# The FFN's first product as 2x2 block products: seven block multiplications for each pair of feature tiles instead of eight

## The chip, the cores and the metric

The kernel runs on one core of one Trainium2 chip. A core has TensorE (PE; its weight loads are listed apart as PEld), VectorE (DVE), ScalarE (ACT), GpSimd (POOL) and the queue SyncE (SP), which here only issues DMAs. The metric is the device time of one execution in microseconds; the median of three runs before the change is 1822.69 us (1821.99 to 1825.63).

## The reference, cut to what matters

Two layers, each a token mixer and then a gated ConvFFN, in float32, over 512 tokens of width 1024. The change touches the FFN's first product:

```
def conv_ffn(x, w_up, conv_w, conv_b, w_down):      # x 512x1024, w_up 1024x5632, w_down 2816x1024
    u = x @ w_up
    u = causal_conv_width_3(u, conv_w) + conv_b     # along the tokens, each feature by itself
    a, b = split(u, 2)
    return (gelu(a) * b) @ w_down
```

## The kernel before

Every float32 matrix product is made of three TensorE products of rounded halves: `split` (L143) writes a rounded high half with ACT (L144) and the rest, source minus high half, with DVE (L145); `mm3` (L147) issues the three matmuls (L149 to L151), each with its own 128x128 stationary tile and a moving operand of up to 512 columns.

Weights come as tiles of 128x1024 float32 (512 KB). `plan_all` (L300) writes their order into a list, `pump` (L125) walks it: it loads a tile into one of 3 `raw` buffers with a DMA on SP, splits it into one of 5 `w` buffers (`wsp`) at high priority, and `weight` (L137) keeps four tiles ready ahead of their use. The order of the instructions on each engine is then set by a list scheduler, by priorities and the dependences; each engine runs its own list in that order and waits where an operand isn't there.

In the FFN (`ffn`, L862) the activations lie transposed in `xT`: features on partitions, 8 tiles of 128 (the K tiles), high and low half, 512 tokens. The 5632 columns of `w_up` are 22 pairs of feature tiles (a tile of the gate's half `a`, and its partner of `b`). A tile is 8 K tiles x 3 matmuls of 512 columns into one PSUM bank (`fm_tile`, L153). The first two pairs run in two halves of 256 tokens, so that they can start before the mixer's last rows are normed. Then `up_pair` (L848) does `conv` (L839) on both tiles (ACT L843: last tap and bias; DVE L844 and L845: the two other taps, read from PSUM), gelu on ACT (L856), the product a*b on DVE (L857) and the split of the result into `gT` (a `u` tile, of which the pool `big` has 21). After 14 pairs the second product is done for these (28 tiles of `w_down`; PSUM added to `x` at L886), then come the other 8 pairs, then `closing` (L810) with the rest of `w_down` and the layer norm.

The lines that the prediction's steps touch: the weights' split (L144, L145), the conv (L843 to L845), the gate (L856, L857), the split of the gate (L144, L145), and the norm (L721, two DVE operands in SBUF, and L292, GpSimd's power of one or eight numbers).

## Time and profile before

| | |
|---|---|
| median of 3 runs | 1822.69 us |
| the profiled execution | 1823.07 us |
| its span, first to last instruction | 1821.4 us |
| granted TensorE clock, mean | 0.998 of 2.4 GHz |
| matmuls | 8286 |
| DVE, ACT, POOL instructions | 2205, 1187, 57 |

The profile is of one execution. Busy time is the union of an engine's instructions; matmuls overlap one another, so their pace is read from the starts of neighbours in the timeline, not from their durations. In a group of instructions the numbers behind the bar are busy us, mean ns of one, and the idle time of the engine just before them with what ended it.

### The profile page before, as it was taken

To read this page: it belongs to the slowest core of one execution; us is meant where nothing else is said; L and a number is where in the kernel's file an instruction comes from. 1 tells how busy PE (TensorE), PEld (TensorE's weight loads), DVE (VectorE), ACT (ScalarE), POOL (GpSimd) and SP (SyncE) were. 2 spreads that over 40 slices of the span, in tenths; PEclk is the share of its full clock that TensorE was granted. 3 is DMA by queue.
4 is the path that set the end of the run, shared out by engine and by line. 5 is a ranking of instruction groups with operands and counts; after the bars stand their busy time and mean duration, and the time that the engine had idled before them with its cause. 6 is when DMAs were issued, how large, how long until landed. Compare 5 with 4: busy or idle time off the path is not lost.

```text
span 1821.4 us, 21842 instructions
## 1 busy us (share of the span) xinstructions
PE 1796.6 (99%) x8286; PEld 1443.6 (79%) x8286; DVE 1183.5 (65%) x2205; ACT 791.4 (43%) x1187; POOL 35.5 (2%) x57
## 2 busy tenths in 40 slices
PE   9999999999999999999999999999999999999997
PEld 6787787888888888888777777778888888888885
DVE  6899867833496653356868997686335865633567
ACT  5744566622334442144356346574222354421441
POOL 0000000000000000000000000000000000000000
PEclk9999999999999999999999999999999999999999
DMA  5122231232452232232631222312325432223233
GB/s 193 64 70 70 70 105 57 66 109 81 137 211 93 94 97 97 94 93 93 210 127 59 70 70 79 96 56 72 105 93 193 131 116 93 93 93 95 96 113 135
DMA packets 57349, 186.17 MB, mean 102 GB/s; under 512 B 6710, under 2 KB 6966, under 8 KB 57244
## 3 DMA queue, kind: packets, MB, share of 16 engines
q1 hardware_dynamic: 51680, 170.74, 28.9%
q10 hardware_dynamic: 4284, 11.94, 1.8%
q0 software_dynamic: 1280, 2.10, 0.5%
q8 instruction: 65, 1.06, 0.2%
q14 instruction: 40, 0.33, 0.1%
HBM read 178.46 MB, written 4.19 MB: 100 GB/s over the span
## 4 chain that ended last, share of the span: by engine, by line
PE 84%; DVE 8%; DMA 3%; ACT 2%; issue 2%; POOL 1%; ACTq 0%; POOLq 0%; DVEq 0%; SPq 0%
PE ps L149 26%; PE ps L151 26%; PE ps L150 26%; DVE w L145 3%; PE ps L476 1%; PE ps L477 1%; ACT w L144 1%; DMA raw<-in_w_down 1%; PE ps L621 1%; POOL rs L292 1%; DMA raw<-in_w_mix_out 1%; DVE m L509 1%; DVE sc L510 1%; PE ps L631 0%; PE ps L728 0%
## 5 line engine op out<-in xcount | busy, mean ns | idle before, releaser
L145 DVE TENSOR_TENSOR w<-raw,w 128x1024 fp32r<-128x1024 f32 (+1 forms) x320 | 387.4, 1215 | 489.9 <-ACT w L144 489.1
L144 ACT CAST w<-raw 128x1024 fp32r<-128x1024 f32 (+1 forms) x320 | 331.8, 1042 | 526.6 <-PE ps L151 430.8
L149 PE MATMUL ps<-xT,w 128*128 128x512 f32 (+2 forms) x1232 | 477.0, 387 | 0.4 <-DVE xT L145 0.4
L151 PE MATMUL ps<-xT,w 128*128 128x512 f32 (+2 forms) x1232 | 473.2, 384 | 0.0
L150 PE MATMUL ps<-xT,w 128*128 128x512 f32 (+2 forms) x1232 | 473.1, 384 | 0.0
L149 PEld LDWEIGHTS ps<-xT,w 128*128 128x128 f32 (+1 forms) x1232 | 231.4, 188 | 48.7 <-DVE xT L145 1.6
L151 PEld LDWEIGHTS ps<-xT,w 128*128 128x128 f32 (+1 forms) x1232 | 231.2, 188 | 48.9
L150 PEld LDWEIGHTS ps<-xT,w 128*128 128x128 f32 (+1 forms) x1232 | 231.4, 188 | 45.9
L149 PE MATMUL ps<-w,u 128*128 128x512 f32 x480 | 190.6, 397 | 4.2 <-DVE u L836 2.6
L150 PE MATMUL ps<-w,u 128*128 128x512 f32 x480 | 189.6, 395 | 0.0
L151 PE MATMUL ps<-w,u 128*128 128x512 f32 x480 | 189.3, 396 | 0.0
L149 PE MATMUL ps<-w,xT 128*128 128x512 f32 x448 | 182.2, 407 | 1.9 <-DVE w L145 1.9
L150 PE MATMUL ps<-w,xT 128*128 128x512 f32 x448 | 178.0, 397 | 0.0
L151 PE MATMUL ps<-w,xT 128*128 128x512 f32 x448 | 177.6, 397 | 0.0
L144 ACT CAST u<-h 128x512 fp32r<-128x512 f32 x108 | 66.8, 621 | 199.8 <-DVE h L857 108.6
L149 PEld LDWEIGHTS ps<-w,u 128*128 128x128 f32 x480 | 90.4, 188 | 28.8 <-DVE u L836 4.3
L151 PEld LDWEIGHTS ps<-w,u 128*128 128x128 f32 x480 | 90.4, 188 | 20.9
L150 PEld LDWEIGHTS ps<-w,u 128*128 128x128 f32 x480 | 90.4, 188 | 20.3
L149 PEld LDWEIGHTS ps<-w,xT 128*128 128x128 f32 x448 | 84.5, 189 | 22.0 <-DVE w L145 2.3
L151 PEld LDWEIGHTS ps<-w,xT 128*128 128x128 f32 x448 | 84.4, 188 | 20.2
L145 DVE TENSOR_TENSOR u<-h,u 128x512 fp32r<-128x512 f32 x108 | 73.9, 687 | 38.0 <-ACT u L144 37.7
L150 PEld LDWEIGHTS ps<-w,xT 128*128 128x128 f32 x448 | 84.6, 189 | 16.3
(198 smaller groups left out, 2134.0 us busy)
## 6 DMA issues: line engine op xcount, KB each, us to landing
raw<-in_w_fm SPq DMA_DIRECT2D x160, 512.0 KB, 3.6
raw<-in_w_down SPq DMA_DIRECT2D x60, 512.0 KB, 3.5
raw<-in_w_tm SPq DMA_DIRECT2D x56, 512.0 KB, 3.5
raw<-in_w_mix_out SPq DMA_DIRECT2D x32, 512.0 KB, 3.6
raw<-in_p_attn SPq DMA_DIRECT2D x8, 512.0 KB, 3.5
u<-in_xT SPq DMA_DIRECT2D x8, 256.0 KB, 4.8
u<-u POOLq DMA_DIRECT2D x16, 128.0 KB, 2.7
u<-in_x ACTq DMA_DIRECT2D x4, 512.0 KB, 4.9
```

The lines of the kernel that those rows point to most:

```text
L144: self.nc.scalar.copy(hi, src)
L145: self.nc.vector.tensor_sub(lo, src, hi.bitcast(F32))
L149: mm(out, lh, rl, start=start, stop=False)
L150: mm(out, ll, rh, start=False, stop=False)
L151: mm(out, lh, rh, start=False, stop=stop)
L292: self.nc.gpsimd.tensor_tensor(r, ve, self.nhalf[:, :n], ALU.pow)
L476: mm(out, q, k, start=True, stop=False)
L477: mm(out, q, kl, start=False, stop=True)
L509: nc.vector.max(m8, sc)
L510: nc.vector.match_replace(sc, m8, sc, TAKEN)
L621: nc.tensor.transpose(ps[:, qb * 128:(qb + 1) * 128], P[qb][:, sb * 128:(sb + 1) * 128], self.ident)
```

## The change

From the third pair on (20 pairs in each layer), a pair's product is a 2x2 block product: the two blocks of rows are the halves of 256 tokens, the inner ones the halves of the 1024 features (4 K tiles each), the two blocks of columns the pair's two feature tiles. Strassen's scheme in Winograd's form makes it with seven products of sums and differences (`b11`, `t2`, `t1`, `t4`, `t3`, `b21`, `b22`), each 4 K tiles x 3 matmuls of 256 columns.

- `factors`: once in a layer, the sums and differences of the activations' blocks, on DVE and GpSimd, and their splits.
- `pair_weights`: a pair's weights come in one DMA of 1 MB; GpSimd makes four sums of 128x512 of them; one split of 128x512 and three of 128x1024 follow. The pair takes three `w` buffers and three `u` tiles.
- `pair_steps`: the seven products go into four PSUM banks; ACT (two copies) and DVE (five differences of 128x256, each with an operand in PSUM) put them together into `ua` and `ub` in SBUF. A pair's first product is issued before the last one of the pair ahead.
- `gate`: the conv's third tap is now a scaling in place on ACT and an add on GpSimd; the gate's low half is made by GpSimd (for the first two pairs, which stay as they were, by DVE).
- The second product runs in four pieces, after pairs 6, 12 and 16 (`down`) and at the end (`closing`), instead of two.
- `raw` is 2 buffers of two tiles each instead of 3 of one; two small scratch tiles of the mixer now come from the pool `half`.

```
 NFM = 36 + 2 * NF
-KA = 14
+DIRECT = 2
...
         self.tiny = pool("tiny", 6)
-        self.wraw = pool("wraw", 3)
+        self.wraw = pool("wraw", 2)
...
     def pump(self, ahead, parts=None):
-        while self.nsp < len(self.seq) and len(self.ready) < ahead:
+        while self.nsp < len(self.seq) and sum(c for _, _, c in self.ready) < ahead:
             key, src, n = self.seq[self.nsp]
             self.nsp += 1
-            raw = self.wraw.tile([128, n], F32, name=self.name("raw"), tag="raw")
+            if n == "pair":
+                self.ready.append((key, self.pair_weights(src), 3))
+                continue
+            raw = self.raw(n)
             self.nc.sync.dma_start(raw.rearrange(src[1], **src[2]) if src[1] else raw, src[0])
             w = self.wsp.tile([128, 2, n], F32R, name=self.name("w"), tag="w")
             with self.tc.high_priority():
                 for c in parts or (slice(0, n),):
                     self.split(w[:, 0, c], w[:, 1, c], raw[:, c])
-            self.ready.append((key, w))
+            self.ready.append((key, w, 1))
 
     def weight(self, key, keep=0):
         self.pump(4 + keep)
-        k, w = self.ready.pop(0)
+        k, w, _ = self.ready.pop(0)
         assert k == key, (k, key)
         return w
+    def pair_weights(self, src):
...
+        self.spare = None
+        raw = self.wraw.tile([128, 2, 1024], F32, name=self.name("raw"), tag="raw")
+        nc.sync.dma_start(raw, src)
+        b11, b21, b12, b22 = (raw[:, f, h * 512:(h + 1) * 512] for f in range(2) for h in range(2))
+        t, r = self.u(F32), self.u(F32)
+        one = self.u()
+        w = [self.wsp.tile([128, 2, 2, 512], F32R, name=self.name("w"), tag="w") for _ in range(3)]
+        with self.tc.high_priority():
+            add = nc.gpsimd.tensor_add
+            add(t[:, 0], b11, b12)
+            add(t[:, 1], t[:, 0], b22)
+            add(r[:, 0], t[:, 1], b21)
+            add(r[:, 1], b12, b22)
+            self.split(one[:, 0], one[:, 1], b11)
+            self.split(w[0][:, 0], w[0][:, 1], t)
+            self.split(w[1][:, 0], w[1][:, 1], r)
+            self.split(w[2][:, 0], w[2][:, 1], raw[:, :, 512:])
+        two = lambda x, j: (x[:, 0, j], x[:, 1, j])
+        return {"b11": (one[:, 0], one[:, 1]), "t1": two(w[0], 0), "t2": two(w[0], 1), "t4": two(w[1], 0),
+                "t3": two(w[1], 1), "b21": two(w[2], 0), "b22": two(w[2], 1)}
...
-        p = self.small([128, HEADS, 16], tag="ra", bufs=1)[:, :heads]
-        q = self.small([128, HEADS, 16], tag="rb", bufs=1)[:, :heads]
+        pq = self.h().rearrange("p (z h d) -> p z h d", z=4, h=HEADS)
+        p, q = pq[:, 0, :heads], pq[:, 1, :heads]
...
-        for m in range(2 * KA):
-            fm(FM["up"] + m)
-        for n in range(2):
...
+        for i in range(NF):
+            m = FM["up"] + 2 * i
+            if i < DIRECT:
+                fm(m)
+                fm(m + 1)
+            else:
+                P((l, "pair", i), a["w_fm"][l, m:m + 2].rearrange("m p c -> p m c"), "pair")
...
-        low = self.small([128, 512], tag="low", bufs=1)
+        low = self.h()
...
-    def conv(self, m, ps):
+    def conv(self, m, ps, also=None):
...
         nc.scalar.activation(c, ps, AF.Identity, scale=w[:, m, 2:3], bias=self.convb[:, m:m + 1])
         nc.vector.scalar_tensor_tensor(c[:, 1:], ps[:, :S - 1], w[:, m, 1:2], c[:, 1:], op0=ALU.mult, op1=ALU.add)
-        nc.vector.scalar_tensor_tensor(c[:, 2:], ps[:, :S - 2], w[:, m, 0:1], c[:, 2:], op0=ALU.mult, op1=ALU.add)
+        if also:
+            nc.scalar.activation(ps, ps, AF.Copy, scale=w[:, m, 0:1])
+            also.tensor_add(c[:, 2:], ps[:, :S - 2], c[:, 2:])
+        else:
+            nc.vector.scalar_tensor_tensor(c[:, 2:], ps[:, :S - 2], w[:, m, 0:1], c[:, 2:], op0=ALU.mult,
+                                           op1=ALU.add)
         return c
 
+    def gate(self, i, pss, also=None):
+        nc = self.nc
+        a, b = (self.conv(2 * i + j, pss[j], also) for j in range(2))
...
-        self.split(g[:, 0], g[:, 1], a)
+        nc.scalar.copy(g[:, 0], a)
+        (also or nc.vector).tensor_sub(g[:, 1], a, g[:, 0].bitcast(F32))
         return g
 
+    def factors(self):
...
+        def whole(eng, t, k):
+            f, x = full(), blk(t, k).bitcast(F32)
+            eng.tensor_add(f, x[:, :, 0], x[:, :, 1])
+            return f
...
+        def halves(f):
+            out = [self.u(F32R, (128, 2, 2, 256)) for _ in range(2)]
+            for j in range(2):
+                self.split(out[j][:, :, 0], out[j][:, :, 1], f[:, 2 * j:2 * j + 2])
+            return lambda k, z: out[k // 2][:, k % 2, z]
...
+        f21 = whole(nc.vector, 1, 0)
+        xb = whole(nc.gpsimd, 0, 0)
+        nc.vector.tensor_sub(xb, f21, xb)
+        f22 = whole(nc.gpsimd, 1, 1)
+        nc.vector.tensor_sub(f21, f22, f21)
+        X["c"] = halves(f21)
+        nc.vector.tensor_sub(f22, f22, xb)
+        X["a"] = halves(f22)
+        f12 = whole(nc.gpsimd, 0, 1)
+        nc.vector.tensor_sub(f12, f22, f12)
+        X["d"] = halves(f12)
+        return X, xb
+
+    def pair_steps(self, l, i, X, out):
+
+        nc = self.nc
+        w = self.weight((l, "pair", i))
...
+        def product(ps, wk, xk, start):
+            wh, wl = w[wk]
+            for k in range(4):
+                c = slice(k * 128, (k + 1) * 128)
+                self.mm3(ps, wh[:, c], wl[:, c], X[xk](k, 0), X[xk](k, 1), start and k == 0, k == 3,
+                         skip_group_check=True)
+        sub = nc.vector.tensor_sub
+        product(al, "b11", "11", True)
+        yield
+        with self.tc.high_priority():
+            nc.scalar.copy(E, al)
+        product(be, "t2", "a", True)
+        with self.tc.high_priority():
+            sub(ub[:, lo], be, E)
+        product(ep, "t1", "c", True)
+        product(ga, "t4", "22", True)
+        product(be, "t3", "b", False)
+        with self.tc.high_priority():
+            sub(W, be, E)
+            sub(ub[:, hi], W, ep)
+            sub(ua[:, hi], ga, W)
+        product(al, "b21", "12", False)
+        with self.tc.high_priority():
+            nc.scalar.copy(ua[:, lo], al)
+        yield
+        product(ep, "b22", "d", False)
+        with self.tc.high_priority():
+            sub(ub[:, lo], ub[:, lo], ep)
+        out[i] = self.gate(i, (ua, ub), nc.gpsimd)
...
+        X, xb = self.factors()
...
+        self.split(self.xT[:, 0:4, 0, 256:], self.xT[:, 0:4, 1, 256:], xb)
+        prev = None
+        for i in range(DIRECT, NF):
+            cur = self.pair_steps(l, i, X, gT)
+            next(cur)
+            if prev:
+                for _ in prev:
+                    pass
+            next(cur)
+            prev = cur
+            if i + 1 in PHASES or i == NF - 1:
+                for _ in prev:
+                    pass
+                prev = None
+            if i + 1 in PHASES:
+                self.down(l, gT, max([0] + [k for k in PHASES if k <= i]), i + 1)
...
+        self.closing(l, "wdB", gT, PHASES[-1], NF, lambda tb: self.norm(tb, g, b, last=l == L - 1))
...
+    def down(self, l, gT, k0, k1):
+
+        nc = self.nc
...
```

DVE's list in the middle of the FFN of layer 0, before (one pair; `h` are the conv's results, `w` the weights' low halves):

```order
L145 TENSOR_TENSOR w_5660<-raw_5658,w_5660 128x1024
L844 SCALAR_TENSOR_TENSOR h_5615<-ps_5590,cw_215,h_5615 128x511
L845 SCALAR_TENSOR_TENSOR h_5615<-ps_5590,cw_215,h_5615 128x510
L145 TENSOR_TENSOR w_5694<-raw_5692,w_5694 128x1024
L844 SCALAR_TENSOR_TENSOR h_5649<-ps_5624,cw_215,h_5649 128x511
L845 SCALAR_TENSOR_TENSOR h_5649<-ps_5624,cw_215,h_5649 128x510
L857 TENSOR_TENSOR h_5615<-h_5615,h_5649 128x512
L145 TENSOR_TENSOR u_5655<-h_5615,u_5655 128x512
```

The same engine and place after the change (one pair; `u_6130` and `u_6131` are GpSimd's sums, L184 is the split's DVE line, `ps` operands are in PSUM):

```order
L964 TENSOR_TENSOR h_6021<-ps_6016,mid_6019 128x256
L888 SCALAR_TENSOR_TENSOR h_6052<-h_5888,cw_215,h_6052 128x511
L184 TENSOR_TENSOR w_6002<-raw_5995,w_6002 128x1024
L901 TENSOR_TENSOR h_6047<-h_6047,h_6052 128x512
L969 TENSOR_TENSOR mid_6019<-ps_6016,mid_6019 128x256
L970 TENSOR_TENSOR h_6021<-mid_6019,ps_6017 128x256
L971 TENSOR_TENSOR h_6020<-ps_6018,mid_6019 128x256
L184 TENSOR_TENSOR w_6133<-u_6130,w_6133 128x1024
L184 TENSOR_TENSOR u_6132<-raw_6128,u_6132 128x512
L888 SCALAR_TENSOR_TENSOR h_6180<-h_6020,cw_215,h_6180 128x511
L978 TENSOR_TENSOR h_6021<-h_6021,ps_6017 128x256
L184 TENSOR_TENSOR w_6134<-u_6131,w_6134 128x1024
```

Five differences from PSUM and two more splits have come in; one conv tap a tile and the gate's low half have gone.

GpSimd's list there (before, its rows of the FFN are the L292 of the norm alone, so only the list after the change is shown):

```order
L891 TENSOR_TENSOR h_5914<-h_5754,h_5914 128x510
L891 TENSOR_TENSOR h_5919<-h_5755,h_5919 128x510
L170 TENSOR_TENSOR u_5997<-raw_5995 128x512
L173 TENSOR_TENSOR u_5998<-raw_5995 128x512
L171 TENSOR_TENSOR u_5997<-u_5997,raw_5995 128x512
L904 TENSOR_TENSOR u_5926<-h_5914,u_5926 128x512
L172 TENSOR_TENSOR u_5998<-u_5997,raw_5995 128x512
```

Seven operations for each pair, all with two inputs in SBUF: four sums of the weights (L170 to L173), the last taps of both tiles (L891), and the gate's low half (L904).

## Rows read from the trace of the kernel before

**Rows 1.** Page, part 1: busy us (share of the span) and instructions of each engine.

```profile
PE 1796.6 (99%) x8286; PEld 1443.6 (79%) x8286; DVE 1183.5 (65%) x2205; ACT 791.4 (43%) x1187; POOL 35.5 (2%) x57
```

**Rows 2.** Page, parts 4 and 2: the chain that ended last; the granted clock.

```profile
PE 84%; DVE 8%; DMA 3%; ACT 2%; issue 2%; POOL 1%; ACTq 0%; POOLq 0%; DVEq 0%; SPq 0%
...
PEclk9999999999999999999999999999999999999999
```

**Rows 3.** Timeline of PE in the FFN: matmuls of 512 columns (start us, us).

```profile
690.25 0.40 PE L149 MATMUL ps<-xT,w 128*128 128x512 f32 x1
...
702.14 0.40 PE L149 MATMUL ps<-w,u 128*128 128x512 f32 x1
```

**Rows 4.** Timeline of PE at the FFN's start: matmuls of 256 columns.

```profile
535.73 0.28 PE L149 MATMUL ps<-xT,w 128*128 128x256 f32 x1
...
541.06 0.28 PE L149 MATMUL ps<-xT,w 128*128 128x256 f32 x1
```

**Rows 5.** Groups of instructions by shape, DVE.

```profile
L145 DVE TENSOR_TENSOR w<-raw,w 128x1024 fp32r<-128x1024 f32 x316 | 385.2, 1223 | 489.9 <-ACT w L144 489.1
L145 DVE TENSOR_TENSOR u<-h,u 128x512 fp32r<-128x512 f32 x108 | 73.9, 687 | 38.0 <-ACT u L144 37.7
...
L844 DVE SCALAR_TENSOR_TENSOR h<-ps,cw,h 128x511 f32<-128x511 f32 x88 | 65.5, 744 | 0.0
L857 DVE TENSOR_TENSOR h<-h,h 128x512 f32<-128x512 f32 x44 | 30.5, 693 | 1.8
...
L145 DVE TENSOR_TENSOR mid<-ps,mid 128x256 fp32r<-128x256 f32 x16 | 6.7, 418 | 2.1 <-ACT mid L144 1.9
```

**Rows 6.** Groups of instructions by shape, ACT.

```profile
L144 ACT CAST w<-raw 128x1024 fp32r<-128x1024 f32 x316 | 329.9, 1049 | 526.0 <-PE ps L151 430.8 <-issue 57.0 <-DMA u<-in_ln_b 10.6
L843 ACT ACTIVATE h<-ps,cb,cw 128x512 f32<-128x512 f32 x88 | 68.2, 775 | 0.0
L144 ACT CAST u<-h 128x512 fp32r<-128x512 f32 x108 | 66.8, 621 | 199.8 <-DVE h L857 108.6 <-DVE h L540 39.9 <-DVE h L702 34.0
L856 ACT ACTIVATE h<-h 128x512 f32<-128x512 f32 x44 | 27.8, 632 | 88.0 <-DVE h L845 88.0
...
L144 ACT CAST mid<-ps 128x256 fp32r<-128x256 f32 x16 | 5.9, 368 | 3.0 <-PE ps L621 2.7
```

**Rows 7.** Groups of instructions by shape, POOL.

```profile
L292 POOL TENSOR_TENSOR rs<-rs,nhalf 128x8 f32<-128x8 f32 x4 | 6.6, 1651 | 383.6 <-DVE rs L291 383.6
L269 POOL MEMSET h<- 96x512 f32 x2 | 1.1, 526 | 304.6 <-DVE h L857 301.1 <-DVE h L239 3.5
...
masks.py:199 POOL TENSOR_SCALAR_AFFINE_SELECT ident<-ident 128x128 f32<-128x128 f32 x1 | 0.3, 293 | 0.0
...
masks.py:197 POOL MEMSET ident<- 128x128 f32 x1 | 0.2, 205 | 0.3 <-POOLq L950 0.3
...
L205 POOL MEMSET h<- 64x1 f32 x1 | 0.1, 93 | 0.0
```

**Rows 8.** Timeline of the norms: DVE's L721 and L145, GpSimd's L292, in three places.

```profile
514.24 0.74 DVE L721 SCALAR_TENSOR_TENSOR u<-u,mv,u 128x512 f32<-128x512 f32 x1
514.41 1.00 POOL L292 TENSOR_TENSOR rs<-rs,nhalf 128x1 f32<-128x1 f32 x1 [270.44 <-DVE rs L291]
...
543.01 0.74 DVE L721 SCALAR_TENSOR_TENSOR u<-u,mv,u 128x512 f32<-128x512 f32 x1
543.24 0.92 POOL L292 TENSOR_TENSOR rs<-rs,nhalf 128x1 f32<-128x1 f32 x1 [6.87 <-DVE rs L291]
...
898.04 0.74 DVE L721 SCALAR_TENSOR_TENSOR u<-u,mv,u 128x512 f32<-128x512 f32 x1
898.21 0.98 POOL L292 TENSOR_TENSOR rs<-rs,nhalf 128x1 f32<-128x1 f32 x1 [12.85 <-DVE rs L291]
898.70 1.22 DVE L145 TENSOR_TENSOR w<-raw,w 128x1024 fp32r<-128x1024 f32 x1
```

**Rows 9.** Page, part 6: the weights' loads.

```profile
raw<-in_w_fm SPq DMA_DIRECT2D x160, 512.0 KB, 3.6
```

More of the change, by code (lines that the diff above doesn't have):

```diff
@@ L41 @@
 NFM = 36 + 2 * NF
-KA = 14
+DIRECT = 2
+PHASES = [6, 12, 16]
 def two_pi_parts():
@@ new lines, in pair_steps @@
+    def pair_steps(self, l, i, X, out):
+        nc = self.nc
+        w = self.weight((l, "pair", i))
+        pools = [self.acc] * 4 if i % 2 else [self.tps, self.tps, self.sps, self.sps]
+        al, be, ep, ga = (self.bank(p)[:, :256] for p in pools)
+        lo, hi = slice(0, 256), slice(256, 512)
+        ew = self.mid().bitcast(F32)
+        E, W = ew[:, 0], ew[:, 1]
+        ua, ub = self.h(), self.h()
+        def product(ps, wk, xk, start):
[27 more added lines that the diff above has]
+        out[i] = self.gate(i, (ua, ub), nc.gpsimd)
@@ L862, in ffn @@
     def ffn(self, l):
         nc = self.nc
-        ws = [self.weight((l, "fm", FM["up"] + m)) for m in range(4)]
-        pss = [self.bank(self.acc) for _ in range(4)]
+        ws = [self.weight((l, "fm", FM["up"] + m)) for m in range(2 * DIRECT)]
+        pss = [self.bank(self.acc) for _ in range(2 * DIRECT)]
         gT = {}
+        X, xb = self.factors()
         for tok in ((0, 256), (256, 512)):
-            for m in range(4):
+            for m in range(2 * DIRECT):
                 self.fm_tile(ws[m], tok, pss[m])
@@ L874, in ffn @@
+        g, b = self.row("ln2_g", l), self.row("ln2_b", l)
+        self.closing(l, "wdB", gT, PHASES[-1], NF, lambda tb: self.norm(tb, g, b, last=l == L - 1))
+        if l < L - 1:
+            self.xs = {}
+            for tb in range(TB):
+                self.xs[tb] = self.dram.tile([128, D], F32, name=f"xs{tb}")
+                nc.scalar.dma_start(self.xs[tb], self.x[tb])
+    def down(self, l, gT, k0, k1):
+        nc = self.nc
         for n in range(2):
             ps = [self.bank(self.acc) for _ in range(TB)]
-            for g in range(KA // 2):
+            for g in range(k0 // 2, k1 // 2):
@@ L881, in ffn @@
                         k = 2 * g + kk
-                        self.mm3(ps[tb], gT[k][:, 0, c], gT[k][:, 1, c], w[:, 0, kk], w[:, 1, kk], k == 0,
-                                 k == KA - 1)
+                        self.mm3(ps[tb], gT[k][:, 0, c], gT[k][:, 1, c], w[:, 0, kk], w[:, 1, kk], k == k0,
+                                 k == k1 - 1)
             for tb in range(TB):
                 f = slice(n * 512, (n + 1) * 512)
-                nc.vector.scalar_tensor_tensor(self.x[tb][:, f], self.x[tb][:, f], ALPHA, ps[tb], op0=ALU.mult,
-                                               op1=ALU.add)
-        for i in range(KA, NF):
-            gT[i] = self.up_pair(l, i)
-        g, b = self.row("ln2_g", l), self.row("ln2_b", l)
-        self.closing(l, "wdB", gT, KA, NF, lambda tb: self.norm(tb, g, b, last=l == L - 1))
-        if l < L - 1:
-            self.xs = {}
-            for tb in range(TB):
-                self.xs[tb] = self.dram.tile([128, D], F32, name=f"xs{tb}")
-                nc.scalar.dma_start(self.xs[tb], self.x[tb])
+                if k0:
+                    nc.vector.tensor_add(self.x[tb][:, f], ps[tb], self.x[tb][:, f])
+                else:
+                    nc.vector.scalar_tensor_tensor(self.x[tb][:, f], self.x[tb][:, f], ALPHA, ps[tb], op0=ALU.mult,
+                                                   op1=ALU.add)
     def run(self):
```

46 lines of the change are left out of this document (26 added, 20 removed).

## The prediction

> **What bounds the kernel now.** First the busy times: PE is busy for 99% of the span, DVE for 65%, ACT 43%, POOL 2% [rows 1]. Then the chain that ended last, to see whether the busy engine is also the one that sets the end: 84% of it is PE, and the granted clock is at full speed throughout [rows 2]. So time is saved only where PE gets less to do, and lost wherever PE begins to wait. A matmul's own duration (0.40 us) overlaps its neighbours' and is no price; the pace is. From the first to the second row of [rows 3] there are 51 matmuls in 11.89 us: 0.2331 us for 512 columns. In [rows 4], 45 matmuls in 5.33 us: 0.1184 us for 256. Half the columns cost 51%, so narrow blocks with a weight load for each lose next to nothing.
>
> **PE's part of the change.** A pair of tiles took 48 x 0.2331 = 11.19 us; it will take 84 x 0.1184 = 9.95 us. For 40 pairs: **-49.7 us**. The second product has as many matmuls as before. If nothing else moved, 1823.07 - 49.7 = 1773 us.
>
> **What each engine gets for a pair**, against PE's new 9.95 us.
> DVE: three low halves of 128x1024 (1.223) and one of 128x512 (0.687), 4.36 us; two conv taps (0.744 each), 1.49; the product, 0.69: together 6.54 us, all with *two operands in SBUF*. Then five differences with one operand in PSUM, at the price of the 128x256 one, 5 x 0.418 = 2.09. In all 8.63 us [rows 5].
> ACT: 3 x 1.049 + 0.621 for the high halves, 2 x 0.368 for the copies, 2 x 0.775 for the conv, two scalings at the gelu's 0.632, gelu 0.632 and 0.621: 8.6 us [rows 6].
> POOL: seven two-operand operations of 128x512. The trace has none of this kind, so their price is put together from [rows 7]: a memset takes 0.205 us for 128 columns and 0.526 for 512, so 0.84 ns for each written element over some 0.1 us of fixed cost; the select, which also reads one operand, takes 0.088 us more for 128 columns, 0.69 ns for each read. Two reads and a write are 2.2 ns, for 512 columns and the fixed part **1.2 us**. The ends: not under 0.53 us (the memset alone), not over 1.65 us (GpSimd's other two-operand operation, a power of eight numbers, the dearest row). I take 1.2, since it is built from rows of the same kind of work. Seven are 8.4 us.
> So each engine by itself fits under 9.95 us. That decides only if they work side by side.
>
> **Do DVE and GpSimd work side by side?** [rows 8] says no, for operations that read two SBUF operands on DVE. GpSimd's power of one number starts 0.16 to 0.23 us behind a L721 (two SBUF operands), and lasts 1.00, 0.92 and 0.98 us: the later it starts, the shorter. Its end stands at 515.41, 544.16 and 899.19, that is 0.43, 0.41 and 0.41 us behind the *end* of L721 (514.98, 543.75, 898.78). The operation ends by the DVE instruction's end and not by its own start: it stood before a read that DVE held. The trace doesn't show the other direction (the L145 that starts under the third one lasts its usual 1.22 us, but one number is no load). For the sum it makes no difference who waits: if one reads at a time, a pair needs 6.54 + 8.4 = **14.9 us** of this shared read, and PE only 9.95.
> The Trainium skill (SBUF — State Buffer, section Who interferes with whom) has the same pair of engines and the same condition, and adds that whoever starts first holds it for the whole instruction; by that DVE would also be held by GpSimd's adds, which no row here shows and the sum doesn't need. Its page GPSIMD Engine Reference (section 3.1) has 4497 ns for an add of 2048 columns; as an estimate from it, 1.12 us for 512, and the sum below would come to 1838 us in place of 1854.
>
> **How much of that reaches PE.** The pieces of the second product give PE work (144 matmuls of 512 columns, 33.6 us; 22.4 us after pair 16) in which the shared read has little to do, so pairs are prepared there. Preparing a pair costs 4.36 + 4 x 1.2 = 9.2 us of it, its gate 2.2 + 3.6 = 5.8. The five weight buffers at three for a pair let 1.67 pairs be ready, 15.3 us. For one layer:
> - Start and pairs 3 to 6. PE: 192 x 0.1184 + 4 x 9.95 = 62.5. Shared read: the activations' sums, five DVE operations of 1.22, six splits of 0.69 and one of 1.22 (11.4), three GpSimd adds of 1024 columns at 2.3 (6.9), the first two pairs' gates (2.8), four pairs (59.8), less the last gate, which lies under the second product (5.8), and the first sums, which are listed ahead of the activations' (4.8): 70.3. PE waits 7.8.
> - Pairs 7 to 12. 6 x 14.94 - 15.3 - 5.8 = 68.5 against 59.7: 8.8. The piece ahead holds 7.3 (splits of w_down) + 5.8 + 15.3 = 28.4 of its 33.6.
> - Pairs 13 to 16. 59.8 - 15.3 - 5.8 = 38.7 against 39.8: 0.
> - Pairs 17 to 22. The shorter piece ahead leaves 22.4 - 4.9 - 5.8 = 11.7 for preparing: 89.6 - 11.7 - 5.8 = 72.1 against 59.7: 12.4.
> That is 29 us a layer, **+58 us**, if the shared read never rests. It will: each add has a fixed part of some 0.1 us (one column costs 0.093 [rows 7]), and 16 pairs in the bound stretches have seven: 11 us a layer, **+22 us**.
> **The sum:** 1823.07 - 49.7 + 58 + 22 = **1854 us**, made against the profiled execution, which lies 0.4 us above the median. At the ends of the add's price the same working gives: 0.53 us, 10.3 us a pair, all hidden, 1773; 1.65 us, 18.1 us a pair, 20 + 23 + 7 + 31 = 82 us a layer, with the fixed parts of all 20 pairs 1966.
>
> **Edits that I cost at nothing, and their cover.** The eight banks added to `x` in two more pieces (16 x 0.69 us of DVE a layer) read PSUM, not the shared read, and lie under the second product; a bank is emptied while the three others still get matmuls. The 1 MB loads hold the same bytes, 512 KB land in 3.6 us [rows 9]; a raw buffer is now free only when GpSimd's sums are made too, so SP waits for POOL and the loads behind it queue, but a load is due two pairs ahead of its use, some 20 to 30 us; if POOL falls back by a whole pair, that cover goes. Scratch from `half` instead of its own tile: in the mixer, under PE. Fewer and later splits ahead of the first block: PE has the first two pairs (22.7 us) meanwhile.
>
> **The rivals.**
> *Side by side, faster.* The read is held only for a moment (the operation in [rows 8] reads one number) and long operations interleave. For it: no row shows DVE held back. Against it: two operands of full rate leave no free cycle, and all ends in [rows 8] follow DVE. Then PE sets the time, with DVE and ACT at 87% of the pair's 9.95 us; the start and the ends of the stretches, where a gate's chain of nine operations stands alone, cost 1 to 2 us each: 1773 + 12 = 1785 us (1773 to 1815). It decides where DVE's rows keep 1.22 us while POOL is busy.
> *A cheap add, no change or a little faster.* The read is shared, but an add takes under 1.05 us. At 0.95 a pair needs 13.2 us, PE waits 4 us a layer and the fixed parts stay: 1823 - 50 + 8 + 22 = 1803 us. The point from which it decides is 1.05, where waits and gain cancel.
> *Lists that wait for each other, much slower.* DVE's list has a difference that waits for PE (L964, L969, L978) ahead of the next pair's splits; where POOL has nothing ready meanwhile, the 2.09 us of differences add to the pair as well: 16 pairs x 2 layers x 2.09 = 67 us more, 1921 us. For it: lists in fixed order. Against: PE runs on four other banks meanwhile.
> *It doesn't do what it says.* 256 columns at the pace of the weight load's listed 0.19 us would eat the gain; [rows 4] shows 0.1184 with a load for each. No chance of its own.
>
> **How the numbers follow.** Less than 0.2% (3.6 us) is about what a measurement of this kernel can't tell from no change. The forecast (the shared read bounds the pair): 0.56; side by side: 0.25; cheap add: 0.12; waiting lists: 0.07. Faster: 0.25 + 0.08 of the cheap add = 0.33. Same: 0.04 of it + 0.03 of the forecast's low end = 0.07. Slower: 0.53 + 0.07 = 0.60. The forecast's own range is 1825 to 1895 us. The range for 8 in 10 goes from 1780 (most of side by side) to 1900 (leaving out most of the waiting lists and the add's dear end).
>
> **What would show it.** Right: POOL busy some 300 to 350 us; its 128x512 rows at 1.2 us or, where they wait, longer; DVE's 128x1024 splits with a mean well over 1.22 us, or starting late; PE idle in pairs 3 to 12 and 17 to 22, ended by DVE L184; the pair's pace 13 to 16 us there and near 10 in pairs 13 to 16. Wrong: DVE's splits at 1.22 us beside a busy POOL, PE at 99% and a pace of 10 us everywhere (side by side); or PE waiting for ACT or a DMA, of which the sum has nothing.

## Result, and the profile after

The changed kernel takes 1939.82 us (median of 4 runs, 1939.57 to 1943.79) against 1824.16 us for the kernel before on the same chip (4 runs, 1821.99 to 1825.89): ratio 1.064, 95% interval 1.062 to 1.066. Slower, as forecast, but by 116 us and not by 31: the forecast of 1854 us and its range (up to 1900) are missed.

The page of the changed kernel, part 1 and the head of part 4 (the chain that ended last), which answer to [rows 1, 2]:

```profile
PE 1796.4 (93%) x9726; PEld 1514.2 (78%) x9726; DVE 1393.8 (72%) x2417; ACT 930.8 (48%) x1433; POOL 476.7 (25%) x343
...
PE 57%; DVE 16%; POOL 12%; ACT 6%; issue 6%; DMA 2%; POOLq 0%; ACTq 0%; DVEq 0%; SPq 0%
```

POOL is busy 25% of the span, yet it and DVE now hold 28% of the chain. What PE waits for, from the view of waits (us in total, times, longest):

```profile
PE ps L188 <- DVE h L964: 31.5, 22, 2.1
PE ps L188 <- DVE h L970: 30.0, 25, 2.4
PE ps L772 <- DVE u L766: 12.4, 3, 6.0
PE ps L188 <- DVE xT L184: 12.2, 5, 5.0
PE ps L189 <- POOL u L904: 11.6, 7, 3.2
```

L964 and L970 are the pair's differences on DVE (each reads a PSUM bank into which PE adds its next product), L766 the norm ahead of the FFN, L904 the low half of a gate. The groups of POOL by shape, which answer to [rows 7], show the adds:

```profile
L891 POOL TENSOR_TENSOR h<-h,h 128x510 f32<-128x510 f32 x80 | 111.2, 1390 | 239.2 <-ACT h L890 239.2
L172 POOL TENSOR_TENSOR u<-u,raw 128x512 f32<-128x512 f32 x40 | 74.3, 1856 | 1.4
...
L904 POOL TENSOR_TENSOR u<-h,u 128x512 fp32r<-128x512 f32 x40 | 57.0, 1425 | 31.0 <-ACT u L903 31.0
```

The mean of the seven operations of a pair runs from 1.39 to 1.86 us; where DVE doesn't hold them up, they take 1.09 (L891) and 1.25 to 1.28 us (the sums, L904). And the groups of DVE, which answer to [rows 5]:

```profile
L184 DVE TENSOR_TENSOR w<-u,w 128x1024 fp32r<-128x1024 f32 x80 | 111.2, 1392 | 81.8 <-ACT w L183 81.8
...
L184 DVE TENSOR_TENSOR u<-raw,u 128x512 fp32r<-128x512 f32 x40 | 59.8, 1494 | 0.9 <-ACT u L183 0.8
L901 DVE TENSOR_TENSOR h<-h,h 128x512 f32<-128x512 f32 x44 | 55.7, 1266 | 42.3 <-POOL h L891 42.3
```

A split of 512 columns takes 1.49 us where it took 0.69, a product 1.27 where it took 0.69. The differences, which read PSUM, keep 0.41 to 0.42. The timeline of DVE and POOL in a pair of the second bound stretch (start, duration) shows who stands behind whom:

```profile
715.46 1.25 POOL L170 TENSOR_TENSOR u<-raw 128x512 f32<-128x512 f32 x1
715.53 1.73 DVE L901 TENSOR_TENSOR h<-h,h 128x512 f32<-128x512 f32 x1 [0.98 <-POOL h L891]
716.68 1.72 POOL L173 TENSOR_TENSOR u<-raw 128x512 f32<-128x512 f32 x1
717.19 0.41 DVE L969 TENSOR_TENSOR mid<-ps,mid 128x256 f32<-128x256 f32 x1
...
720.75 1.23 DVE L184 TENSOR_TENSOR w<-u,w 128x1024 fp32r<-128x1024 f32 x1 [2.36 <-ACT w L183]
720.85 2.28 POOL L172 TENSOR_TENSOR u<-u,raw 128x512 f32<-128x512 f32 x1
721.89 1.78 DVE L184 TENSOR_TENSOR u<-raw,u 128x512 fp32r<-128x512 f32 x1
```

L901 starts under POOL's L170 and ends 0.55 us behind its end (717.26 and 716.71); L172 starts under a split and ends 1.15 us behind it (723.13 and 721.98), about its own price; the next split starts under L172 and ends 0.54 us behind it. So one reads at a time, in both directions. L969 has an operand in PSUM; it runs under L173 and is not slowed.

Where the time went, layer 0, by windows of the changed kernel (us of the window, then busy time and count of PE, PEld, DVE, ACT and POOL, the granted clock as a share of full speed, DMA share and GB/s):

```profile
547.00:555.00 8.00, 1.99 (x11) 1.83 (x10) 5.93 (x8) 1.81 (x3) 4.26 (x2) 0.71 0.00 0
555.00:628.00 73.00, 58.07 (x436) 56.40 (x435) 66.37 (x71) 41.33 (x61) 37.52 (x22) 0.91 0.23 73
628.00:667.50 39.50, 36.31 (x146) 29.05 (x146) 22.46 (x22) 12.38 (x16) 23.60 (x16) 0.91 0.23 80
667.50:744.00 76.50, 64.89 (x505) 63.00 (x504) 54.27 (x66) 44.34 (x64) 42.18 (x30) 0.96 0.26 83
```

| stretch of layer 0, us | PE's need | forecast | measured |
|---|---|---|---|
| start, pairs 3 to 6 | 62.5 | 70.3 | 93.1 |
| second product, piece 1 | 33.6 | 33.6 | 39.4 |
| pairs 7 to 12 | 59.7 | 68.5 | 76.6 |
| piece 2 | 33.6 | 33.6 | 34.3 |
| pairs 13 to 16 | 39.8 | 39.8 | 46.5 |
| piece 3 | 22.4 | 22.4 | 29.8 |
| pairs 17 to 22 | 59.7 | 72.1 | 76.0 |
| closing part | 33.6 | 33.6 | 33.5 |
| sum | 344.9 | 373.9 | 429.2 |

PE's need is its matmuls at full pace. The forecast's 11 us a layer for fixed parts come on top of its 373.9. What is left, 429.2 - 384.9 = 44.3 us a layer, is the miss to within 3 us: 88.6 for two layers, 85.8 measured. The table counts some 6 us a layer that PE waits in the FFN of the kernel before too (376.0 us for a need of 369.6), and leaves out some 5 us that are lost behind the closing part. From the FFN's start to the same matmul of the next layer (at 983.1 us, before at 925.5) layer 0 takes 448.0 us against 389.8: 58.2 more, where the forecast has 29 + 11 - 24.9 = 15.1. That is a miss of 43.1 a layer.

Not all of it is waiting. PE in the first piece of the second product (L904 is the low half of a gate), and the window behind that wait:

```profile
639.82 0.40 PE L188 MATMUL ps<-w,u 128*128 128x512 f32 x1
643.40 0.80 PE L189 MATMUL ps<-w,u 128*128 128x512 f32 x1 [3.19 <-POOL u L904]
...
645.27 0.63 PE L190 MATMUL ps<-w,u 128*128 128x512 f32 x1
645.70 0.63 PE L188 MATMUL ps<-w,u 128*128 128x512 f32 x1
```

```profile
643.40:649.30 5.90, 5.90 (x14) 4.66 (x15) 3.09 (x4) 0.62 (x1) 5.90 (x4) 0.50 0.25 102
```

PE stands 3.2 us, and behind it the granted clock is at the lower of its two levels (0.50 of full speed, 1.2 GHz): neighbours start 0.43 us apart in place of 0.233. In the FFN of layer 0, 126 matmuls start at this level. At 0.427 us for 512 columns and 0.213 for 256 (0.233 and 0.118 at full speed) they take some 14 us more, an estimate from their count: 4.9 in the start, 4.7 in the pieces, 4.2 in pairs 7 to 22. It is an upper bound, since a slower PE in a pair waits less for DVE. In the kernel before no matmul of the FFN starts at the lower level.

### The profile page after: what moved, and what is told of

It is laid out like the page before. It is cut to its first block, busy times and chain, and to the rows that moved or that the text cites. A ratio compares the mean times of both kernels' runs of the same rounds, so it can differ in the third digit from the quotient of the medians.

```text
span 1937.8 us, 25250 instructions
## 1 busy us (share of the span) xinstructions
PE 1796.4 (93%) x9726; PEld 1514.2 (78%) x9726; DVE 1393.8 (72%) x2417; ACT 930.8 (48%) x1433; POOL 476.7 (25%) x343
## 3 DMA queue, kind: packets, MB, share of 16 engines
q1 hardware_dynamic: 50976, 168.64, 24.9%
q8 instruction: 76, 1.25, 0.3%
## 4 chain that ended last, share of the span: by engine, by line
PE 57%; DVE 16%; POOL 12%; ACT 6%; issue 6%; DMA 2%; POOLq 0%; ACTq 0%; DVEq 0%; SPq 0%
PE ps L188 18%; PE ps L189 17%; PE ps L190 17%; POOL h L891 5%; DVE w L184 3%; DVE u L184 3%; ACT w L183 2%; POOL u L173 2%; ACT h L890 2%; POOL u L171 2%; DVE h L888 2%; POOL u L170 2%; POOL u L904 1%; PE ps L520 1%; PE ps L521 1%
## 5 line engine op out<-in xcount | busy, mean ns | idle before, releaser
L184 DVE TENSOR_TENSOR w<-raw,w 128x1024 fp32r<-128x1024 f32 (+1 forms) x276 | 352.6, 1283 | 266.5 <-ACT w L183 265.5
L183 ACT CAST w<-raw 128x1024 fp32r<-128x1024 f32 (+1 forms) x276 | 285.0, 1039 | 344.4 <-PE ps L190 289.9
L188 PE MATMUL ps<-xT,w 128*128 128x256 f32 (+2 forms) x1072 | 369.3, 345 | 43.7 <-DVE h L964 31.5
L189 PE MATMUL ps<-xT,w 128*128 128x256 f32 (+2 forms) x1072 | 362.6, 338 | 0.0
L190 PE MATMUL ps<-xT,w 128*128 128x256 f32 (+2 forms) x1072 | 361.6, 338 | 0.0
L331 POOL TENSOR_TENSOR rs<-rs,nhalf 128x1 f32<-128x1 f32 (+1 forms) x20 | 22.3, 1113 | 1033.4 <-DVE rs L330 1027.7
L188 PEld LDWEIGHTS ps<-xT,w 128*128 128x128 f32 (+1 forms) x1072 | 208.8, 195 | 69.3 <-DVE h L964 36.0
L188 PE MATMUL ps<-u,w 128*128 128x256 f32 (+1 forms) x672 | 217.4, 324 | 39.3 <-DVE h L970 30.0
L190 PEld LDWEIGHTS ps<-xT,w 128*128 128x128 f32 (+1 forms) x1072 | 208.7, 195 | 20.1
L189 PEld LDWEIGHTS ps<-xT,w 128*128 128x128 f32 (+1 forms) x1072 | 209.1, 195 | 16.6
L189 PE MATMUL ps<-u,w 128*128 128x256 f32 (+1 forms) x672 | 213.6, 318 | 0.0
L190 PE MATMUL ps<-u,w 128*128 128x256 f32 (+1 forms) x672 | 212.9, 318 | 0.0
L189 PE MATMUL ps<-w,u 128*128 128x512 f32 x480 | 194.3, 405 | 11.6 <-POOL u L904 11.6
L188 PEld LDWEIGHTS ps<-u,w 128*128 128x128 f32 x672 | 129.6, 193 | 54.7 <-DVE h L970 35.7
L891 POOL TENSOR_TENSOR h<-h,h 128x510 f32<-128x510 f32 x80 | 111.2, 1390 | 239.2 <-ACT h L890 239.2
L184 DVE TENSOR_TENSOR w<-u,w 128x1024 fp32r<-128x1024 f32 x80 | 111.2, 1392 | 81.8 <-ACT w L183 81.8
L183 ACT CAST w<-u 128x1024 fp32r<-128x1024 f32 x80 | 83.9, 1049 | 138.7 <-PE ps L190 78.8
```

The lines of the kernel that those rows point to most:

```text
L183: self.nc.scalar.copy(hi, src)
L184: self.nc.vector.tensor_sub(lo, src, hi.bitcast(F32))
L188: mm(out, lh, rl, start=start, stop=False, **kw)
L189: mm(out, ll, rh, start=False, stop=False, **kw)
L190: mm(out, lh, rh, start=False, stop=stop, **kw)
L331: self.nc.gpsimd.tensor_tensor(r, ve, self.nhalf[:, :n], ALU.pow)
```

## Experiments

All times stand beside runs of the kernel before on the same chip, 1822.2 to 1824.0 us. Where one time and no interval is given, the kernel was run once; the kernel before spreads over some 4 us (1822.0 to 1825.9). Theory 1 is the shared read; theory 2 that the pair's steps wait for one another in the engines' fixed lists.

### Writes only

Every add of a pair on GpSimd becomes two memsets of the same columns, in the same place of the list:

```
-            add(t[:, 0], b11, b12)
...
+            for x in (t[:, 0], t[:, 1], r[:, 0], r[:, 1]):
+                nc.gpsimd.memset(x, 0.5)
+                nc.gpsimd.memset(x, 0.5)
...
-            also.tensor_add(c[:, 2:], ps[:, :S - 2], c[:, 2:])
+            also.memset(ps[:, :S - 2], 0.5)
+            also.memset(c[:, 2:], 0.5)
...
```

> Each of GpSimd's seven additions of a pair is replaced by two memsets of the same width in the same place of its list (0.52 us each in the trace before, so 1.04 us against the addition's 1.09 to 1.28 us alone); they write SBUF and read nothing, and the last tap, the gate's low half and the sums are left out. DVE's and ACT's work and order stay. Theory 1, the shared read: DVE and GpSimd no longer hold each other up, DVE's splits go back to 1.22 us, a pair takes 10 to 11 us in place of 15, the kernel 1790 to 1825 us. Theory 2, waiting lists (the product a*b stands in DVE's list ahead of the differences that release PE, and waits for a chain through ACT and GpSimd): chain and order are the same, a pair stays at 13.5 to 15 us, the kernel over 1890 us.

Measured: 1805.31 us. A group of POOL, and the window of pairs 7 to 12, of this run:

```profile
L172 POOL MEMSET u<- 128x512 f32 x160 | 79.5, 527 | 0.0
```

```profile
646.00:705.40 59.40, 59.40 (x503) 59.40 (x502) 44.49 (x66) 43.43 (x64) 26.54 (x54) 1.00 0.32 107
```

PE doesn't pause: six pairs in 59.8 us, 9.97 each. POOL is busy 26.5 us in the window and does no harm: DVE's 128x1024 splits take at most 1.23 us beside a memset. The hand-overs are the same, and so is DVE's list, but for two neighbouring splits; PE's waits for L964 and L970 are gone, and DVE waits for POOL's tap 4.9 us in the run (42.3 in the changed kernel). It is the *read* that costs. The start still takes 77.0 us; the sums of the activations, which were left on GpSimd, are in it.

### Without the weight sums; without any add of a pair on GpSimd

The first leaves out the four sums, the second the gate's adds too (in `pair_weights` `t = r = raw[:, :, :512]`, in `conv` no third tap, in `gate` no low half).

> The four sums of a pair's weights on GpSimd are left out (the splits that read them read raw weights of the same size), the gate's three additions stay. Theory 1: the shared read has 6.54 + 3 x 1.25 = 10.3 us in a pair, near PE's 9.95: a pair 10.3 to 11.5 us, the kernel 1800 to 1840 us. Theory 2: the gate's chain is untouched, a pair 13 to 15 us, the kernel over 1880 us.

> All seven of GpSimd's additions of a pair are left out (as in the run without sums, and the conv's third tap isn't added, and the high half of the gate stands for its low one). ACT and the matmuls stay, DVE loses nothing of a pair. Both theories: a pair at PE's 9.95 us or little over it, the kernel 1785 to 1805 us; this measures what the first blocks of a layer and the ends of the stretches cost without GpSimd. If it stays over 1830 us, both are wrong and DVE or ACT alone bounds the pair.

Measured: 1849.96 and 1807.53 us. The first is 10 us over theory 1's range and 30 under theory 2's, the second 2.5 us over its own. Pairs 7 to 12 take 64.9 and 59.8 us. With three adds left on GpSimd (L886, a tap, at 1219 ns) a pair takes 10.8 us; their shared read is 6.54 + 2 x 1.09 + 1.26 = 10.0. DVE waits for the tap 45.5 us in this run, no less than in the changed kernel (42.3): that wait alone doesn't make 15 us of a pair. Reads and writes gone together cost as little as writes alone (1805).

### The gate one pair later

A pair's gate is issued after the first six of the seven block products of the pair behind it (a `yield` ahead of `self.gate(...)`).

> Nothing is left out: the gate of a pair is written after the next pair's products, so that in DVE's list the product a*b comes some 5 us later and no longer waits for GpSimd in front of the differences that release PE. Theory 1: the reads are the same, a pair stays at 14.5 to 15 us, the kernel 1915 to 1945 us. Theory 2: a pair loses its wait of some 2 us or more, 12.5 to 13 us, the kernel 1860 to 1890 us.

Measured: 1987.67 us, outside both, 48 us slower than the changed kernel. DVE's differences now wait too (L978 for PE 41.2 us, L964 for POOL's tap 14.3), and L901 waits more for the tap (51.7, in the changed kernel 42.3): issuing later moves the wait, and takes no read away. But the reads are the same seven adds and the time is not: the sum of the reads is a floor, and the order of the lists decides what comes on top.

### Gate, sums, or both on DVE

Three complete kernels: `self.gate(i, (ua, ub))` without `nc.gpsimd`; `add = nc.vector.tensor_add`; both.

> The whole computation; the pair's gate (two taps, the last difference) goes back from GpSimd to DVE, the four sums stay on GpSimd. Theory 1 (one shared read, one instruction at a time): a pair takes the sum of DVE's two-operand work (6.54 + two taps 1.49 + one difference 0.69 = 8.72 us) and of four sums at 1.27 (5.08), 13.8 us in place of 15.1; of the stretches of pairs 3 to 22 some 1.3 us for each of 40 pairs at most, and the pieces of the second product wait less for their last gate: 1880 to 1905 us. Theory 2 (the changed kernel is late because a gate passes between two engines, each step waiting in a list): no hand-over is left in the gate, so the pace falls to near 10.5 to 11.5 us and the time to 1830 to 1850. Rival 3 (GpSimd's own speed is the bound: 8.5 us busy): GpSimd has 5.1 us a pair, PE's 9.95 us sets the pace, 1805 to 1815.

> The whole computation; the four weight sums go from GpSimd to DVE, the gate's three operations stay on GpSimd. Theory 1 (one shared read): 6.54 + 4 x 0.69 + 2 x 1.09 + 1.26 = 12.7 us a pair; 1860 to 1885 us. If DVE's list alone counted (two-operand 9.3 + differences 2.1): 11.4 us, 1835 to 1850. Theory 2 (hand-overs of the gate): no change of the gate, so the waits of the pieces for the last gate (6 to 7 us each) stay and the pace is 13 to 15 us: 1900 to 1935.

> The whole computation with nothing on GpSimd: sums and gate on DVE. No read is shared, so the bound is DVE's own busy time for a pair, 8.72 + 4 x 0.69 + 2.09 = 13.6 us. Theory 1 has this and the run with the gate alone on DVE within 0.5 us a pair of each other (13.6 and 13.8): handing four sums to GpSimd would buy nothing at all. If the two engines worked side by side even in part, the run with the sums on GpSimd is clearly the quicker of the two. 1875 to 1905 us.

Measured: 1888.17, 1897.94 and 1841.11 us. The gate was in theory 1's range; the sums missed theirs by 13 us and ended 2 us under theory 2's; and all on DVE is 34 us under its range: the sum of row durations held it to be no better than the gate alone (13.6 against 13.8 us a pair), and it is 47 us quicker. Two things are shown. First, the timeline of DVE with nothing of a pair on GpSimd:

```profile
671.67 0.69 DVE L170 TENSOR_TENSOR u<-raw 128x512 f32<-128x512 f32 x1
672.27 0.42 DVE L970 TENSOR_TENSOR h<-mid,ps 128x256 f32<-128x256 f32 x1
672.60 0.69 DVE L171 TENSOR_TENSOR u<-u,raw 128x512 f32<-128x512 f32 x1
673.20 0.42 DVE L971 TENSOR_TENSOR h<-ps,mid 128x256 f32<-128x256 f32 x1
```

Neighbours start 0.60 and 0.33 us apart for 0.69 and 0.42: back to back they overlap by some 0.08, which the nineteen instructions of a pair turn from 13.6 into some 11.9 us (an estimate from these distances; the pace, not the duration, is the price, as it is on PE). And an add that takes 0.60 us on DVE holds the read for 1.25 to 1.28 on GpSimd. Second, with the sums on DVE and the gate on GpSimd, DVE still stands before the gate's product:

```profile
DVE h L901 <- POOL h L891: 48.8, 36, 2.0
```

In its list the differences come behind L901, and PE waits for L964 23.7 us and for L970 26.2. With the gate on DVE this wait is gone, and PE's for L964 falls from 31.5 to 4.4 (for L970 it stays, 28.4). So theory 2's waits exist, but as what the shared read makes of them: with writes only, in nearly the same lists, PE's vanish and DVE's fall to 4.9 us.

### Without the activations' sums

`X["a"], X["c"], X["d"]` become plain blocks; `factors` issues nothing.

> Leaves out the sums of the activations and their splits: the five products that need them take a plain block of the activations instead, so the output is another. It measures the start of the FFN. By my own sum these operations hold the shared read for 18 us; the stretch from the start of the FFN to the end of pair 6 took 93.0 us against PE's 62.5. Theory a (the activations' sums are the start's extra cost): 72 to 78 us, 30 to 40 us less in all, near 1905. Theory b (the first pair's weight sums, which stand ahead of the last norm in the lists of GpSimd and DVE, hold PE up): the hole of 5 to 6 us at the last norm stays, and the stretch is still 83 us or more: 1915 to 1925.

Measured: 1912.50 us, 27 less, between the two ranges. The start with pairs 3 to 6 takes 83.8 us, 9 less, and piece 1 34.4 (39.4). PE's hole at the last norm stays, and grows to 10 us (545.9 to 555.9).

### The norm first

The changed kernel with the norms ahead of the FFN issued at high priority: the first pair's two splits come behind most of the last norm in DVE's list.

> The whole computation; the changed kernel with the norms before the FFN listed ahead of what has been prepared for the first block pair: on DVE the two first splits (w and u, which wait for GpSimd's sums) come behind the reciprocal root and the first half of the last norm. If the place in the list makes the hole (8 us between the products of the first 384 tokens and the rest, 1.4 us in the kernel before): it shrinks to 3 to 5 us, and the time by 6 to 10 us, to 1930 to 1934. If the shared read slows the norm's own operations: the hole stays at 6 to 8 us, 1936 to 1941.

Measured: 1940.98 us, no gain: PE's waits for the last norm (L766 in the changed kernel) sum to 6.3 us in layer 0, where they were 6.0. The place in the list alone is not the cause. The timeline of DVE and POOL in that hole:

```profile
541.51 1.28 POOL L170 TENSOR_TENSOR u<-raw 128x512 f32<-128x512 f32 x1
...
543.99 1.70 POOL L171 TENSOR_TENSOR u<-u,raw 128x512 f32<-128x512 f32 x1
...
547.00 2.80 POOL L920 TENSOR_TENSOR u<-xT 128x1024 f32<-128x1024 f32 x1
```

```profile
541.56 1.24 DVE L332 TENSOR_TENSOR rs<-rs 128x1 f32<-128x1 f32 x1 [0.44 <-POOL rs L331]
...
544.50 1.21 DVE L333 TENSOR_TENSOR rs<-rs,rs 128x1 f32<-128x1 f32 x1
...
547.52 2.30 DVE L335 TENSOR_TENSOR rs<-rs,rs 128x1 f32<-128x1 f32 x1
```

Operations of **one column** last 1.24, 1.21 and 2.30 us, to within 0.03 us of the end of the add they started under (542.79, 545.69, 549.80); the same happens in layer 1. In the changed kernel the two of them that meet no add take 0.15 and 0.16, and the first 0.34. In this order a chain of tiny two-operand operations on DVE pays a whole add at each step. L334 with a single operand, in between, under the add L172, takes 0.14.

In the changed kernel's own order the hole has another maker:

```profile
547.74 1.32 DVE L184 TENSOR_TENSOR w<-u,w 128x1024 fp32r<-128x1024 f32 x1 [2.26 <-ACT w L183]
548.99 2.82 DVE L184 TENSOR_TENSOR u<-raw,u 128x512 fp32r<-128x512 f32 x1
551.74 0.15 DVE L333 TENSOR_TENSOR rs<-rs,rs 128x1 f32<-128x1 f32 x1
```

Here the norm's next step, L333, stands behind two splits: DVE waits 2.26 us for the first one's high half, which waits for GpSimd's sums, and the second takes 2.82 us beside an add. In the kernel before that step (L294) starts at 545.80. One order loses to the list, the other to the adds.

### Block products in some of the pairs

PE gains 1.24 us for each block pair, DVE needs some 11.9 us for one (all on DVE) and 6.2 for a direct pair, estimates from the distances above; so some pairs stay direct (`BLOCK` counts them from 0). The activations' sums are made after the fourth pair and the gate is on DVE. In all but the first kernel the sums are on DVE too.

```
+BLOCK = set(range(7, 22, 2))
...
+            if i == 4:
+                X, _ = self.factors()
+            if i in BLOCK:
...
+            else:
+                pss = [self.fm_tile(self.weight((l, "fm", FM["up"] + 2 * i)))]
...
```

> The whole computation. Block products only in every other pair from 7 to 21 (eight of 22 a layer), between them pairs as in the kernel before; the activations' sums are made after pair 3 and not at the start; the gate is on DVE, the weight sums stay on GpSimd; the second product in pieces after pairs 6, 10, 14 and 18. Theory 1 (one shared read): a block pair and a direct pair need 13.8 + 6.8 = 20.6 us of the read against PE's 9.95 + 11.19 = 21.1, so PE is just the bound and 16 x 1.24 = 20 us are gained, less what the factors and the pieces' ends cost: 1806 to 1822. Start: no hole at the last norm beyond that of the kernel before. If lists rather than the sum were the limit, waits at the block pairs' gates as in the changed kernel: 1825 to 1850.

> The whole computation; as the run with block products in every other pair, but the weight sums and the activations' sums on DVE too, nothing on GpSimd. In the run with all on DVE instructions that follow each other on DVE began 0.60 us apart for one of 0.69 and 1.14 for one of 1.23, so a block pair takes some 11.9 us of DVE and a direct pair 6.2: 18.1 us against PE's 21.1. Theory 1: PE is the bound with 3 us to spare for every two pairs; 1802 to 1812, below the kernel before by about 1%. If the gate's chain or the extra pieces of the second product cost what they did in the changed kernel (5 us each): 1825 or more.

> The whole computation; as the run with every other pair and all sums on DVE, with three block pairs in four (7 to 9, 11 to 13, 15 to 17, 19 to 21; twelve a layer). DVE: 3 x 11.9 + 6.2 = 41.9 us for four pairs against PE's 3 x 9.95 + 11.19 = 41.0, and DVE catches up under the pieces of the second product (22.4 us of PE after every four pairs). Theory 1: PE stays the bound, 24 x 1.24 = 30 us gained: 1793 to 1806. If DVE can't prepare ahead there (weight buffers, three to a block pair): 1806 to 1820, no better than every other pair.

Measured: 1836.63; 1824.43 (ratio 1.0006, interval 0.9996 to 1.0016); 1852.92 (1.017, 1.015 to 1.018). All missed theory 1's range on the slow side; the first lies in the range written for the lists, the second 0.6 us short of the one for the pieces' cost, the third above both. Moving the sums from GpSimd to DVE is worth 12 us between the first two. In the second run two block and two direct pairs take 42.3 us, PE's need to the tenth. The hole at the last norm is 1.4 us, as before. What it gained it lost at the layer's end; the window 896 to 930 us of the kernel before, and of this run:

```profile
896.00:930.00 34.00, 33.36 (x154) 25.71 (x153) 28.70 (x61) 10.34 (x14) 2.95 (x3) 1.00 0.50 169
```

```profile
896.00:930.00 34.00, 26.51 (x107) 19.90 (x106) 29.07 (x67) 9.22 (x14) 2.95 (x3) 0.85 0.37 131
```

With pieces after pairs 6, 10, 14 and 18 the closing part has four pairs, 48 matmuls a half, to cover the norms of the half before, where the kernel before has eight. PE waits for the next layer's input, and the granted clock falls to 0.85. With three block pairs in four, each piece but the first ends on a block pair, and PE stands before its gate:

```profile
PE ps L189 <- ACT u L904: 24.6, 10, 7.1
```

The last two put this right: pieces after 6, 10 and 14 with every other pair, so that the closing part has eight pairs again; and pieces after 8 and 14, each ended by a direct pair, with ten block pairs in a layer. The second's lines against the run with three in four:

```
-PHASES = [6, 10, 14, 18]
+PHASES = [8, 14]
-BLOCK = {i for i in range(7, 22) if i % 4 != 2}
+BLOCK = {6, 8, 9, 11, 12, 14, 15, 17, 18, 20}
```

> The whole computation; as the run with block products in every other pair and all sums on DVE, but the second product in pieces after pairs 6, 10 and 14, so that its closing part takes eight pairs as in the kernel before, not four. In the run with pieces after 6, 10, 14 and 18 the pairs kept PE's pace (42.3 us for two block and two direct pairs) and layer 0 was 9 us ahead of the kernel before at the end of the second product, but lost it between 900 and 928 us, where PE waits for the norms that four pairs (11.2 us a half) don't cover. If that is all: 1804 to 1812. If the block pairs lose time elsewhere: 1818 or more.

> The whole computation; all sums on DVE, ten block pairs a layer (6, 8, 9, 11, 12, 14, 15, 17, 18, 20), each piece of the second product ends with a direct pair, pieces after pairs 8 and 14, the closing part takes eight. PE gains 20 x 1.24 = 25 us; DVE needs 2 x 11.9 + 6.2 = 30.0 us for three pairs against PE's 31.1. If only the pieces' ends and the closing part cost: 1800 to 1808. If a block pair that follows a block pair waits for its differences (as at the ends of the pieces in the run with three in four, some 5 us each): 1815 to 1830.

Measured: 1804.09 us (ratio 0.989, interval 0.988 to 0.991) and **1802.07** (0.988, 0.986 to 0.990), both as expected, 19.5 and 21.5 us under the kernel before. The first differs from the 1824.43 us of the same block pairs in the pieces and the longer closing part; what one piece fewer gives by itself was not measured. Part 1 of the page of the last:

```profile
PE 1772.7 (98%) x9006; PEld 1462.7 (81%) x9006; DVE 1328.6 (74%) x2473; ACT 838.4 (47%) x1279; POOL 35.5 (2%) x57
```

Of the 24.8 us that twenty block pairs save PE, 21.5 arrive; of the 19.8 of sixteen, 19.5.

## Why the prediction was wrong

**Right.** The sign, and the mechanism: DVE's two-operand instructions and GpSimd's share one read, one at a time. Runs with writes only and without adds take it away, and the pairs then keep PE's pace (9.97 us, 9.95 forecast). The Trainium skill (SBUF — State Buffer, section SBUF: two separate sides) has that whoever starts first holds it for the whole instruction; the rows at 715 and 720 us and the one-column operations agree, in both directions. PE's part was right too, and nearly the price: an add 1.25 to 1.28 against 1.2, a pair in the middle of a bound stretch 15.1 us from L964 to L964 against 14.94. "Side by side" and "a cheap add" fall with that. Of the signs, POOL is busier than forecast (476.7 us against 300 to 350, since its rows hold its waits too), and PE's waits in the pairs are ended by L964 and L970, not by L184.

**Wrong: how much of it is hidden.** The step that failed is "How much of that reaches PE". It counts the shared read as one sum to fill each stretch with, and the chains in it as free. By the table, for a layer:
- *The start*, +22.8 us (70.3 forecast, 93.1 measured). PE stands still three times, 15.8 us in all. The first time, 6.0 us, is at the last norm: "the first sums, which are listed ahead of the activations'" were taken off as hidden, but the splits that wait for them stand in DVE's list ahead of the norm's last steps (the rows at 547 us). Between PE's products the hole is 8.1 us there (546.9 to 555.0) against 1.35 in the kernel before, 6.8 more. The two others, 4.8 and 5.0 us, end with splits of the activations' sums (L184 of `u` and of `xT`); the forecast has these sums as a part of what fills the stretch, and not as a chain that PE stands before. Leaving them out takes 9 us off the stretch. Waits in the pairs (some 6 us), the lower clock (some 5) and the norm's transposes on PE (some 2) make up most of the rest of the 30.6 us above PE's need, of which 7.8 were forecast.
- *The pieces of the second product*, +13.9 (39.4 + 34.3 + 29.8 against 33.6 + 33.6 + 22.4). "the last gate, which lies under the second product" was subtracted from every stretch; but a piece needs that gate, and its chain passes through ACT, GpSimd and DVE. PE waits for GpSimd's low half (L904) 11.6 us in the run. In the first piece that wait is 3.2 us of the 5.8 that are lost, and the lower clock behind it the other 2.6.
- *Pairs 7 to 22*, +18.7 (8.1, 6.7 and 3.9). What the five weight buffers "let 1.67 pairs be ready, 15.3 us", and the last gate, 5.8, were taken off the first two stretches, 21.1 us of each, and 17.5 off the third. Six pairs at 15.1 us are 90.6, and pairs 7 to 12 took 76.6, so 14.0 us were hidden; pairs 13 to 16 hid 13.9, pairs 17 to 22 14.6. In these stretches DVE stands before L901 (42.3 us in the run), with the differences behind it, and PE before the differences (61.5 in the run). How much of what was not hidden is due to these waits, and how much to weights that weren't ready, was not measured; the run without the weight sums has the wait at L901 too, and pairs of 10.8 us. The rival "lists that wait for each other" was right that something could come on top, but not where: its wait, of differences for PE, is 16.3 us in the run (L969 6.2, L978 10.1), and that its 1921 us lie nearest to the result is luck.
- *The granted clock.* The prediction reads it as full "throughout" [rows 2] and has no term for it. In the changed kernel it is 0.975 on average (before 0.998), and at most 14 of the 44 us a layer are matmuls at the lower level. They are in the three items above.
- *The fixed parts*, -11. This term was not there: the adds' own 1.25 to 1.28 us holds it, and the pace of 15.1 leaves nothing more.

22.8 + 13.9 + 18.7 - 11 = 44.4 us a layer.

**Also wrong, on the other side:** DVE's part of a pair was a sum of durations. Back to back its instructions overlap by 0.08 us, so DVE alone does everything in some 11.9 us a pair and not in 13.6. The later forecast for the version with nothing on GpSimd, made with the same sum, was too slow by 34 us, and hid that some of the gain can be had.

**Still open:** why the run with the sums on DVE and the gate on GpSimd is 10 us above the run the other way round, though its sum of the read is smaller (12.7 against 13.8 us); its waits at L901 (48.8 us) fit, but no run took these waits alone.

## What to carry to other kernels

Work given to an idle GpSimd is paid on DVE where both read SBUF and DVE's instructions have two operands there: measure an add by what it takes from them (here 1.27 us for one that costs DVE itself 0.60), and look above all at chains of short DVE operations, which paid a whole add at each step in the run with the norm first. Such a sum gives a floor: what waits before or behind each stretch, and what the clock does after a wait, comes on top. A saving on the busiest engine is worth having only as far as the next engine's pace allows: here, with nothing of a pair on GpSimd, ten block pairs of 22 in a layer gained 1.2% where twenty lost 0.9%; with the adds on GpSimd twenty lost 6.4%. A stretch of the bound engine that covers something (a norm, a last gate) must be kept as long as what it covers.

## What the runs showed of the hardware that the prediction did not have

- GpSimd's memsets cost DVE nothing (1805 us with 14 of them a pair), its adds of the same columns hold DVE's two-operand instructions for 1.25 to 1.28 us each, even one of a single column (1.24 us under an add of 512 columns, 2.30 under one of 1024, in place of 0.16).
- DVE instructions with an operand in PSUM (0.41 to 0.42 us) and a one-column operation with a single SBUF operand (0.14) went unhindered beside busy adds.
- Neighbours on DVE start 0.08 to 0.09 us before the end of the one ahead.
- After PE had stood 3.2 us, its granted clock was at 1.2 GHz for the next 14 matmuls of 512 columns (0.427 us apart), then at 2.4 GHz again (0.233).
